# Convolution taps that read by token from SBUF, and modulation steps outside the down-products, in a two-block transformer kernel

## The chip, the cores and the metric

The kernel runs on one core of one Trainium2 chip. The metric is the device time of one execution in microseconds, as a median over runs. Before the change it is 2077.81 us (three runs, 2076.61 to 2079.95). One more execution was recorded with a profile; its own time is in the table below.

## The reference

Everything is float32, 256 tokens of width 2048. The first block is attention and a gated MLP with a causal depthwise convolution of width 3 between its two products. The second block is modulated: one vector c gives six vectors of 2048 through the matrix w_ada (2048 x 12288), and a second vector c_ctx gives the two that the context needs. Cut to what matters here:

```
def rmsnorm(x, g):                                   # rms_norm alike
    return x * rsqrt(mean(x * x, -1) + EPS) * g

def causal_dwconv(u, w, b):                          # CONV_WIDTH = 3
    up = jnp.pad(u, ((0, 0), (CONV_WIDTH - 1, 0), (0, 0)))
    y = b
    for kk in range(CONV_WIDTH):
        y = y + up[:, kk:kk + S] * w[kk]
    return y

# first block: x (1, 256, 2048), D_FF = 5632
h = rmsnorm(x, pre_mix_g); proj = h @ w_in           # sliding-window and forgetting attention on proj
x = x + rmsnorm(mix @ w_out, post_mix_g)
h = rmsnorm(x, pre_ffn_g)
u = causal_dwconv(h @ w_up, conv_w, conv_b)          # 2 x 5632 wide
gate, val = jnp.split(u, 2, axis=-1)
y = (gelu(gate, approximate=True) * val) @ w_down
x = x + rmsnorm(y, post_ffn_g)

# second block
m = silu(c) @ w_ada + b_ada                          # 6 x 2048; c_ctx alike for ctx
h  = rms_norm(x, norm_attn_w) * (1 + sc_a) + sh_a
hc = rms_norm(ctx, norm_attn_w) * (1 + csc_a) + csh_a
x = x + g_a * (concat([attention(h, hc), pool(h)]) @ w_out)
hm = rms_norm(x, norm_mlp_w) * (1 + sc_m) + sh_m
x = x + g_m * (square(relu(hm @ w_mlp_up)) @ w_mlp_down)
return rms_norm(x, final_norm_w)
```

## The kernel before, in words

**Groups.** All large products run one after the other on TensorE (PE). The program is a list of groups, each a product of the activations with one column stripe of one weight matrix: the first block's projections, wo_a and wo_b (its output product), up0 to up10 (w_up, 1024 columns each, 512 of the gate and 512 of the value), dn0, dn2, ... dn8 (w_down), then the second block: ckv and kv, q, u, wo2 and the MLP's mup and mdn. A down-product takes two halves of 1024 output columns, called dn00 and dn01 for dn0. The order is up0, up1, up2, dn0, up3, up4, dn2, up5, up6, dn4, up7, up8, dn6, up9, up10, dn8: a down-product follows two up groups, so the last of them has its convolution while the down-product runs. Within a group one unit is one block of 128 weight rows. An up group has 16 units; a half of dn0 to dn6 has 8, a half of dn8 has 12. The last block of a group is made one output bank after the other, so the weights of its last unit are wanted earlier than its place says.

**Three passes and the split.** Each product is made in three passes, high x high, high x low and low x high. The weights arrive as 1 MB transfers of two units from the queue of SP into one of four buffers `raw`; ACT writes the high part (L190, `hi`, four buffers), and VectorE (DVE) the rest (L202, `lo` = raw - hi, four buffers, 128x1024 per unit). So DVE must make one `lo` per unit, and PE waits where it is late.

**Side work.** After each unit `tick()` issues one more step of the side work of the group before (a list given to `later`), and on the ticks that the table `PACE` names one step of `ada_side()`, the modulation. Such a step is one pass of DVE over 128 rows of w_ada, multiplied with silu(c) and summed: L641 for c, L638 for c_ctx (only for the first 32 of 96 row blocks). There are 128 of them in the program. The rows come through the same SP queue into the same four `raw` buffers, 1 MB each, and the load for the next step is issued with the L641 step before. A down-product's groups had fill steps at ticks 5, 8 and 2, 5, 8 of their halves.

**The convolution.** `up(g).after` holds it. PE's products stand in four PSUM banks per group with the tokens in an order in which even and odd ones alternate (`evens` reads them back). For each of 8 blocks of 128 channels ACT multiplies by the last tap and adds the bias (L1002, PSUM to SBUF), and DVE adds the two others with L1006 on all but the first tokens that the shifted view reaches, and with L1009 on 1 or 2 columns left over: 16 of L1006 and 16 of L1009 per up group. Then gelu (L1014, ACT), the product (L1017, DVE) and the split of the result (L1023 ACT, L1024 DVE). L1036 and L1038 add the down-products to the block's sum.

**What sets the order.** Within one engine instructions run in a fixed order, and the order is made ahead of time by a list scheduler from the steps as they are issued. An instruction that waits holds all behind it on its engine. Tiles come from pools that rotate: `P4` (p4) has 10 buffers of 4096 bytes per partition. It holds the tap results, the split results and the junk output of L638.

**Warm-up.** `warm_mix` (L356 to L372) issues 60 matmuls (10 on each of six operand pairs) ahead of up0 and 30 ahead of the second block's mup0, while PE waits for a norm. Their result is not used.

## Time and profile before

| | |
|---|---|
| median of three runs | 2077.81 us (2076.61 to 2079.95) |
| profiled execution, its own time | 2074.69 us |
| its span in the trace | 2072.9 us |
| PE busy | 2030.2 us, 98% |
| DVE busy | 1594.8 us, 77% |
| ACT busy | 1078.6 us, 52% |
| POOL busy | 40.4 us, 2% |

The span runs from the first to the last instruction of the profiled execution; 1.8 us of the execution's time lie outside of it. A view of groups gives, for each kind of instruction, the sum of the busy time, the mean duration of one, and behind the second bar the idle time of the engine ahead of them with what ended it. The timeline gives an instruction's start and duration, and in brackets the idle time ahead of it. A duration is longer than the distance to the next start, since instructions of one engine overlap a little at their ends: a `lo` shows as 1.22 us and is followed after 1.14.

### The profile page before, as it was taken

Reading aid. Unit: us, or ns where it says so; the run is one execution under the profiler, and the core shown is the slowest. Engines: PE = TensorE matmul, PEld = TensorE weight load, DVE = VectorE, ACT = ScalarE, POOL = GpSimd, SP = SyncE. Lnnn points to the kernel's source line nnn. Section 1 sums busy time; section 2 is a strip of 40 time slices with the busy share of each in tenths; the row PEclk is TensorE's granted clock in tenths of the full one; section 3 lists DMA queues with packets and bytes.
Section 4 is the critical chain, followed back from the end, with each engine's and each line's share of the span. In section 5 each row is a group of like instructions: output and inputs, shape, how many; then the busy total and the mean of one; then the engine's idle time right before and its main releaser. Section 6 shows DMA issues by size and latency. Waiting matters only on the chain.

```text
span 2072.9 us, 35204 instructions
## 1 busy us (share of the span) xinstructions
PE 2030.2 (98%) x14344; PEld 1885.6 (91%) x14344; DVE 1594.8 (77%) x2271; ACT 1078.6 (52%) x1559; POOL 40.4 (2%) x58
## 2 busy tenths in 40 slices
PE   8999999999999999999999999999999999999997
PEld 7998988998998999989889978889999999999986
DVE  6787788799789788897899798876657667566577
ACT  5556575555454554545557467455544434444444
POOL 0001000000000000000000000000000000000000
PEclk9999999999999999999999999999999999999999
DMA  8753676566767779888887854765667676666673
GB/s 310 283 192 136 162 226 242 209 245 244 274 236 253 276 267 333 292 310 292 284 291 249 310 189 143 200 186 192 234 246 264 224 277 238 216 204 203 202 241 106
DMA packets 120961, 491.39 MB, mean 237 GB/s; under 512 B 8736, under 2 KB 12640, under 8 KB 107360
## 3 DMA queue, kind: packets, MB, share of 16 engines
q1 hardware_dynamic: 120800, 489.16, 68.4%
q8 instruction: 112, 1.84, 0.3%
q14 instruction: 49, 0.40, 0.1%
HBM read 484.90 MB, written 2.13 MB: 235 GB/s over the span
## 4 chain that ended last, share of the span: by engine, by line
PE 85%; DVE 8%; DMA 3%; ACT 2%; issue 2%; POOL 0%; POOLq 0%; ACTq 0%; SPq 0%; DVEq 0%
PE b_up L326 21%; PE b_mup L326 17%; PE b_mdn L326 16%; PE b_dn L326 5%; PE b_qk L326 4%; PE b_wo_a L326 4%; DVE lo L202 3%; PE b_v L326 2%; DMA raw<-in_w_ada 2%; PE b_qa L326 2%; PE b_q L326 2%; PE b_wo_p L326 2%; PE b_wo_b L326 2%; PE b_u L326 1%; DVE raw L641 1%
## 5 line engine op out<-in xcount | busy, mean ns | idle before, releaser
L190 ACT CAST hi<-raw 128x1024 fp32r<-128x1024 f32 (+2 forms) x716 | 726.9, 1027 | 724.7 <-PE b_mup L326 166.7
L202 DVE TENSOR_TENSOR lo<-raw,hi 128x1024 fp32r<-128x1024 f32 (+2 forms) x716 | 845.7, 1198 | 314.1 <-ACT hi L190 311.1
L326 PE MATMUL b_up<-a,hi 128*128 128x256 f32 x2816 | 473.7, 276 | 0.0
L326 PEld LDWEIGHTS b_up<-a,hi 128*128 128x128 f32 x2816 | 428.9, 192 | 0.2
L326 PE MATMUL b_up<-a,lo 128*128 128x256 f32 x1408 | 387.2, 275 | 0.0
L326 PE MATMUL b_mup<-a,hi 128*128 128x256 f32 x2048 | 344.4, 275 | 1.3 <-ACT a L428 1.3
L326 PEld LDWEIGHTS b_mup<-a,hi 128*128 128x128 f32 x2048 | 311.3, 192 | 2.0 <-ACT a L428 1.6
L326 PE MATMUL b_mdn<-hi,p 128*128 128x512 f32 x1024 | 304.7, 379 | 0.0
L326 PE MATMUL b_mup<-a,lo 128*128 128x256 f32 x1024 | 281.5, 275 | 0.0
L326 PEld LDWEIGHTS b_up<-a,lo 128*128 128x128 f32 x1408 | 270.5, 192 | 0.0
L641 DVE SCALAR_TENSOR_TENSOR raw<-raw,srow 128x2048 f32<-128x2048 f32 x96 | 219.5, 2286 | 58.2 <-DMA raw<-in_w_ada 58.2
L326 PEld LDWEIGHTS b_mdn<-hi,p 128*128 128x128 f32 x1024 | 193.0, 189 | 27.1
L326 PE MATMUL b_dn<-hi,p 128*128 128x512 f32 x704 | 210.9, 383 | 0.0
L326 PEld LDWEIGHTS b_mup<-a,lo 128*128 128x128 f32 x1024 | 196.6, 192 | 0.0
L326 PE MATMUL b_mdn<-lo,p 128*128 128x512 f32 x512 | 194.0, 379 | 0.0
L326 PEld LDWEIGHTS b_dn<-hi,p 128*128 128x128 f32 x704 | 133.9, 191 | 18.8
L326 PE MATMUL b_dn<-lo,p 128*128 128x512 f32 x352 | 134.9, 386 | 10.6 <-DVE lo L202 10.6
L326 PEld LDWEIGHTS b_mdn<-lo,p 128*128 128x128 f32 x512 | 96.8, 189 | 13.7
L638 DVE SCALAR_TENSOR_TENSOR p<-raw,srow 128x2048 bf16<-128x2048 f32 x32 | 73.2, 2289 | 22.0 <-DMA raw<-in_w_ada 22.0
L326 PE MATMUL b_qk<-a,hi 128*128 128x256 f32 x512 | 89.7, 280 | 0.0
L326 PEld LDWEIGHTS b_dn<-lo,p 128*128 128x128 f32 x352 | 67.1, 191 | 23.8 <-DVE lo L202 14.3
L1006 DVE SCALAR_TENSOR_TENSOR p<-b_up,vecs,p 128x254 f32<-128x254 f32 (+1 forms) x176 | 82.2, 472 | 1.0 <-ACT p L1002 0.9
(263 smaller groups left out, 2568.2 us busy)
## 6 DMA issues: line engine op xcount, KB each, us to landing
raw<-in_w_ada SPq DMA_DIRECT2D x96, 1024.0 KB, 6.6
raw<-in_w_up SPq DMA_DIRECT2D x88, 1024.0 KB, 5.0
raw<-in_w_mlp_up SPq DMA_DIRECT2D x64, 1024.0 KB, 5.0
raw<-in_w_mlp_down SPq DMA_DIRECT2D x64, 1024.0 KB, 5.5
raw<-in_w_in SPq DMA_DIRECT2D x50, 1024.0 KB, 6.0
raw<-in_w_down SPq DMA_DIRECT2D x44, 1024.0 KB, 6.6
raw<-in_w_out SPq DMA_DIRECT2D x32, 512.0 KB, 6.7
raw<-in_w_out SPq DMA_DIRECT2D x16, 1024.0 KB, 6.4
```

Source lines behind the costliest of these rows:

```text
L190: nc.scalar.copy(h, r)
L202: self.dve.tensor_tensor(out=l, in0=r, in1=h.bitcast(F32), op=ALU.subtract)
L326: self.mm = self.pe.matmul(dst, lhsT, rhs, start=first and n == 0 and m == 0, stop=last and n == len(prog) - 1 and m == 2, skip_group_chec ...
L638: self.dve.scalar_tensor_tensor(out=junk, in0=r, scalar=1.0, in1=self.srow[1], op0=ALU.mult, op1=ALU.mult, accum_out=self.adac[:, f:f + 1])
L641: self.dve.scalar_tensor_tensor(out=r, in0=r, scalar=1.0, in1=self.srow[0], op0=ALU.mult, op1=ALU.mult, accum_out=self.ada[:, f:f + 1])
L1006: self.dve.scalar_tensor_tensor(out=o, in0=evens(p)[:, :, 0:128 - n], scalar=cw(t, 2 - n), in1=o, op0=ALU.mult, op1=ALU.add)
```

## The change

Three things change together.

1. `PACE`: the down-products dn0 to dn8 have no fill ticks any more; the odd ups from up3 have seven (4, 6, ... 16) in place of three, the even ones six in place of five. The number of fill ticks between up0 and dn8 falls from 72 to 68; what is left of the modulation runs in later groups, as it did.
2. The convolution: ACT copies each up group's four banks to two SBUF tiles of 4 x 258 columns by token (`take`, four instructions per group), whose first two columns POOL has set to zero. ACT's first tap and both DVE taps read there, at whole width. The 16 instructions on 1 or 2 columns go, and the banks are free after the copies. p4 gets 12 buffers of 4128 bytes (10 x 4096 before).
3. `warm_mix`: the same number of matmuls, 60 and 30, with other stationary operands (strided by 4, 8 and 16 columns, one column broadcast, shifted slices) and one moving operand for all.

```diff
@@ -31,8 +31,8 @@
 
 
 PACE = dict(v=3, kva=3, qa=4, qk=5, wo_a=2, wo_b=3, ckv=99, kv=2, u=6, q=7, wo2_p=2, wo2_a=99, mup=99, mdn=4)
-PACE.update({f"up{i}": (6, 8, 12, 13, 16) if i < 2 else (7, 10, 15) if i % 2 else (8, 9, 11, 13, 15) for i in range(11)})
-PACE.update({f"dn{i}{half}": ((5, 8), (2, 5, 8))[half] for i in range(0, 10, 2) for half in range(2)})
+PACE.update({f"up{i}": (6, 8, 12, 13, 16) if i < 2 else (4, 6, 8, 10, 12, 14, 16) if i % 2 else (8, 9, 10, 11, 13, 15) for i in range(11)})
+PACE.update({f"dn{i}{half}": () for i in range(0, 10, 2) for half in range(2)})
 
 
 WARM = dict(up0=0, mup0=1)
@@ -114,7 +114,7 @@
         self.raw_p = P("raw", 4)
         self.w_p = P("w", 4)
         self.a8_p = P("a8", 8)
-        self.p4_p = P("p4", 10)
+        self.p4_p = P("p4", 12)
         self.row_p = P("row", 1)
         self.dram_p = P("dram", 1, space=bass.MemoryType.DRAM)
         self.p2_p = P("p2", 6)
@@ -362,10 +362,9 @@
 
         bk = self.bank("warm")
         x = x.rearrange("p k t -> p (k t)")
-        w = x[:, 1024:1152]
-        at = lambda o, d: x[:, o:o + 2 * d].rearrange("p (a b) -> p b a", a=2)[:, 0:128]
-        kinds = (((w, at(0, 128)), (w, at(0, 256)), (w, at(16, 128)), (w, at(48, 128)), (w, at(0, 512)), (x[:, 1024:1280:2], at(0, 128))),
-                 ((w, at(8, 128)), (w, at(0, 136)), (w, at(0, 192))))[kind]
+        w = ((x[:, 1024:1536:4], x[:, 1024:2048:8], x[:, 0:2048:16], x[:, 1024:1025].to_broadcast([128, 128]), x[:, 1028:1156], x[:, 1032:1160]),
+             (x[:, 1040:1168], x[:, 1056:1184], x[:, 0:1920:15]))[kind]
+        kinds = [(v, halves(x[:, 0:256])) for v in w]
         with self.tc.issue_after(after.ins):
             for lhsT, rhs in kinds:
                 for _ in range(10):
@@ -993,20 +992,25 @@
                 gs[g] = out = [None, None]
                 gv = []
 
+                ps = []
+
+                def take(i):
+
+                    if not ps:
+                        ps.extend(self.P4([128, 4, 258]) for _ in range(2))
+                        for t in ps:
+                            nc.gpsimd.memset(t[:, :, 0:2], 0.0)
+                    for t, bank in zip(ps, (banks[i // 2], banks[2 + i // 2])):
+                        ac.copy(t[:, i:i + 2, 2:258].rearrange("p j (a b) -> p j a b", a=2), evens2(bank))
+
                 def taps(s, i):
                     if not gv:
                         gv.extend(self.P4([128, 4, 256]) for _ in range(2))
                     t = 44 * s + 4 * g + i
-                    p = banks[2 * s + i // 2][:, 256 * (i % 2):256 * (i % 2) + 256]
-                    d = gv[s][:, i]
-                    ac.activation(rows2(d), evens(p), AF.Identity, scale=cw(t, 2), bias=cw(t, 3))
+                    p, d = ps[s][:, i], gv[s][:, i]
+                    ac.activation(d, p[:, 2:258], AF.Identity, scale=cw(t, 2), bias=cw(t, 3))
                     for n in (1, 2):
-
-                        o = rows2(d)[:, :, n:128]
-                        self.dve.scalar_tensor_tensor(out=o, in0=evens(p)[:, :, 0:128 - n], scalar=cw(t, 2 - n), in1=o,
-                                                      op0=ALU.mult, op1=ALU.add)
-                        o = d[:, 128:128 + n]
-                        self.dve.scalar_tensor_tensor(out=o, in0=evens(p)[:, 0, 128 - n:128], scalar=cw(t, 2 - n), in1=o,
+                        self.dve.scalar_tensor_tensor(out=d, in0=p[:, 2 - n:258 - n], scalar=cw(t, 2 - n), in1=d,
                                                       op0=ALU.mult, op1=ALU.add)
 
                 def act(i):
@@ -1023,7 +1027,8 @@
                     ac.copy(hi, val)
                     self.dve.tensor_tensor(out=lo, in0=val, in1=hi.bitcast(F32), op=ALU.subtract)
 
-                self.later(*[lambda i=i: (taps(0, i), taps(1, i)) for i in range(4)],
+                take(0)
+                self.later(*[lambda i=i: (i or take(2), taps(0, i), taps(1, i)) for i in range(4)],
                            *[lambda f=f, i=i: f(i) for i in (0, 2) for f in (act, split)])
             return Group(f"up{g}", 16, 1024, self.loader(a["w_up"], 0, 1024 * g, 1024), a_banks(8), lambda k: ht["xs"](k),
                          before=up_before if g == 0 else None, prep=(lambda b: ht["need"](b + 3)) if g == 0 else None,
```

In the changed kernel the lines move a little: `lo` stays L202, the modulation steps are L637 and L640, the taps L1011 (ACT) and L1013 (DVE).

**DVE where dn0 begins, before.** `lo_5481` is the first `lo` of dn0, `lo_5512` the second; `adac` and `ada` mark modulation steps, `b_up` taps of up2:

```order
L638 SCALAR_TENSOR_TENSOR p_763_5449,adac<-raw_5389,srow_353 128x2048
L202 TENSOR_TENSOR lo_5481<-raw_5332,hi_5455 128x1024
L641 SCALAR_TENSOR_TENSOR raw_5389,ada<-raw_5389,srow_385 128x2048
L202 TENSOR_TENSOR lo_5512<-raw_5332,hi_5483 128x1024
L1006 SCALAR_TENSOR_TENSOR p_784_5582<-b_up_5011,vecs,p_784_5582 128x2x127
L1009 SCALAR_TENSOR_TENSOR p_784_5582<-b_up_5011,vecs,p_784_5582 128x1
L1006 SCALAR_TENSOR_TENSOR p_784_5582<-b_up_5011,vecs,p_784_5582 128x2x126
L1009 SCALAR_TENSOR_TENSOR p_784_5582<-b_up_5011,vecs,p_784_5582 128x2
L1006 SCALAR_TENSOR_TENSOR p_784_5582<-b_up_5012,vecs,p_784_5582 128x2x127
L1009 SCALAR_TENSOR_TENSOR p_784_5582<-b_up_5012,vecs,p_784_5582 128x1
```

The same place after the change (`lo_5468` and `lo_5498` are the first two of dn0):

```order
L637 SCALAR_TENSOR_TENSOR p_762_5375,adac<-raw_5345,srow_353 128x2048
L202 TENSOR_TENSOR lo_5468<-raw_5316,hi_5442 128x1024
L640 SCALAR_TENSOR_TENSOR raw_5345,ada<-raw_5345,srow_385 128x2048
L637 SCALAR_TENSOR_TENSOR p_774_5496,adac<-raw_5436,srow_353 128x2048
L202 TENSOR_TENSOR lo_5498<-raw_5316,hi_5470 128x1024
L1013 SCALAR_TENSOR_TENSOR p_791_5576<-p_776_5524,vecs,p_791_5576 128x256 x4
L202 TENSOR_TENSOR lo_5554<-raw_5379,hi_5532 128x1024
L202 TENSOR_TENSOR lo_5556<-raw_5379,hi_5534 128x1024
L1013 SCALAR_TENSOR_TENSOR p_792_5577<-p_777_5525,vecs,p_792_5577 128x256
```

Two modulation steps of dn0 now stand ahead of the second `lo`; before, one stood there and another behind the seventh. The taps are one instruction each, and `lo` stand between them.

**SP around the change from up9 to up10, before.** A row is a 1 MB transfer, `in_w_ada` one of the modulation, `in_w_up` one of two units of weights:

```order
L628 DMA raw_10199<-in_w_ada 128x2048
L390 DMA raw_10203<-in_w_up 128x2x1024
L390 DMA raw_10261<-in_w_up 128x2x1024
L628 DMA raw_10290<-in_w_ada 128x2048
L390 DMA raw_10322<-in_w_up 128x2x1024
L390 DMA raw_10380<-in_w_up 128x2x1024
L628 DMA raw_10437<-in_w_ada 128x2048
L390 DMA raw_10465<-in_w_up 128x2x1024
L390 DMA raw_10503<-in_w_up 128x2x1024
L390 DMA raw_10583<-in_w_up 128x2x1024
```

After the change:

```order
L389 DMA raw_10183<-in_w_up 128x2x1024
L627 DMA raw_10212<-in_w_ada 128x2048
L389 DMA raw_10244<-in_w_up 128x2x1024
L627 DMA raw_10273<-in_w_ada 128x2048
L389 DMA raw_10305<-in_w_up 128x2x1024
L627 DMA raw_10334<-in_w_ada 128x2048
L627 DMA raw_10391<-in_w_ada 128x2048
L389 DMA raw_10399<-in_w_up 128x2x1024
L389 DMA raw_10437<-in_w_up 128x2x1024
L389 DMA raw_10511<-in_w_up 128x2x1024
```

Among ten transfers four are now the modulation's, one to one with the weights' and the last two next to each other; before there were three, with two of the weights between them.

**DVE where dn6 begins, before.** `lo_9576` and `lo_9607` are its first two, `lo_9655` and `lo_9657` the next:

```order
L641 SCALAR_TENSOR_TENSOR raw_9482,ada<-raw_9482,srow_385 128x2048
L202 TENSOR_TENSOR lo_9576<-raw_9425,hi_9550 128x1024
L647 TENSOR_TENSOR ada<-ada,vecs 128x16
L202 TENSOR_TENSOR lo_9607<-raw_9425,hi_9578 128x1024
L1006 SCALAR_TENSOR_TENSOR p_1255_9675<-b_up_9103,vecs,p_1255_9675 128x2x127
L1009 SCALAR_TENSOR_TENSOR p_1255_9675<-b_up_9103,vecs,p_1255_9675 128x1
L641 SCALAR_TENSOR_TENSOR raw_9544,ada<-raw_9544,srow_385 128x2048
L1006 SCALAR_TENSOR_TENSOR p_1255_9675<-b_up_9103,vecs,p_1255_9675 128x2x126
L1009 SCALAR_TENSOR_TENSOR p_1255_9675<-b_up_9103,vecs,p_1255_9675 128x2
L1006 SCALAR_TENSOR_TENSOR p_1256_9676<-b_up_9105,vecs,p_1256_9676 128x2x127
L1009 SCALAR_TENSOR_TENSOR p_1256_9676<-b_up_9105,vecs,p_1256_9676 128x1
L202 TENSOR_TENSOR lo_9655<-raw_9486,hi_9635 128x1024
```

After the change (`lo_9515`, `lo_9546`, `lo_9600`, `lo_9602` are the first four):

```order
L202 TENSOR_TENSOR lo_9515<-raw_9361,hi_9489 128x1024
L640 SCALAR_TENSOR_TENSOR raw_9390,ada<-raw_9390,srow_385 128x2048
L640 SCALAR_TENSOR_TENSOR raw_9422,ada<-raw_9422,srow_385 128x2048
L646 TENSOR_TENSOR ada<-ada,vecs 128x16
L202 TENSOR_TENSOR lo_9546<-raw_9361,hi_9517 128x1024
L1013 SCALAR_TENSOR_TENSOR p_1274_9622<-p_1261_9572,vecs,p_1274_9622 128x256 x4
L202 TENSOR_TENSOR lo_9600<-raw_9426,hi_9580 128x1024
L202 TENSOR_TENSOR lo_9602<-raw_9426,hi_9582 128x1024
L640 SCALAR_TENSOR_TENSOR raw_9483,ada<-raw_9483,srow_385 128x2048
L1013 SCALAR_TENSOR_TENSOR p_1275_9623<-p_1262_9573,vecs,p_1275_9623 128x256 x3
L202 TENSOR_TENSOR lo_9630<-raw_9487,hi_9606 128x1024
```

Three modulation steps now stand ahead of the fifth `lo`, where one stood behind the second and another further down, behind the seventh.

## Rows read from the trace of the kernel before

**Rows 1.** The page: engines, and the chain that ended last.

```profile
PE 2030.2 (98%) x14344; PEld 1885.6 (91%) x14344; DVE 1594.8 (77%) x2271; ACT 1078.6 (52%) x1559; POOL 40.4 (2%) x58
PE 85%; DVE 8%; DMA 3%; ACT 2%; issue 2%; POOL 0%; POOLq 0%; ACTq 0%; SPq 0%; DVEq 0%
```

**Rows 2.** Windows (us; busy PE, PEld, DVE, ACT, POOL; PEclk, DMA): dn0–dn8, mdn.

```profile
496.15:542.32 46.17, 43.67 (x195) 37.33 (x193) 43.22 (x66) 25.25 (x33) 0.00 (x0) 0.96 0.73 260
628.08:671.02 42.94, 41.71 (x195) 36.21 (x193) 42.80 (x68) 22.06 (x27) 0.00 (x0) 1.00 0.72 247
756.78:800.16 43.38, 41.70 (x194) 36.21 (x193) 41.38 (x64) 21.21 (x26) 0.00 (x0) 1.00 0.82 299
885.92:928.31 42.39, 41.71 (x194) 36.22 (x193) 41.15 (x66) 21.48 (x26) 0.00 (x0) 1.00 0.82 301
1014.07:1087.48 73.41, 68.47 (x323) 58.37 (x322) 67.11 (x105) 43.88 (x71) 3.31 (x2) 0.98 0.83 281
1556.96:1598.40 41.44, 41.44 (x195) 36.29 (x193) 31.29 (x31) 19.70 (x21) 0.00 (x0) 1.00 0.73 264
```

**Rows 3.** The same view of up4 and up7.

```profile
585.20:628.08 42.88, 42.88 (x387) 42.88 (x386) 37.15 (x53) 21.29 (x26) 0.00 (x0) 1.00 0.64 233
800.16:843.04 42.88, 42.88 (x385) 42.87 (x384) 33.25 (x39) 18.69 (x21) 0.00 (x0) 1.00 0.87 315
```

**Rows 4.** Timeline of PE where dn0, dn4, dn8 and ckv wait.

```profile
515.71 0.48 PE L326 MATMUL b_dn<-lo,p 128*128 128x512 f32 x1 [1.89 <-DVE lo L202]
517.83 1.06 PE L326 MATMUL b_dn<-hi,p 128*128 128x512 f32 x2
775.46 0.48 PE L326 MATMUL b_dn<-lo,p 128*128 128x512 f32 x1 [1.68 <-DVE lo L202]
1035.93 0.79 PE L326 MATMUL b_dn<-lo,p 128*128 128x512 f32 x1 [3.13 <-DVE lo L202]
1089.90 0.38 PE L326 MATMUL b_ckv<-a,lo 128*128 128x256 f32 x1 [2.04 <-DVE lo L202]
```

**Rows 5.** Timeline of DVE in dn4 ahead of its eighth lo.

```profile
771.46 0.47 DVE L1006 SCALAR_TENSOR_TENSOR p<-b_up,vecs,p 128x252 f32<-128x252 f32 x1
771.85 0.21 DVE L1009 SCALAR_TENSOR_TENSOR p<-b_up,vecs,p 128x2 f32<-128x2 f32 x1
771.98 2.28 DVE L641 SCALAR_TENSOR_TENSOR raw<-raw,srow 128x2048 f32<-128x2048 f32 x1
774.18 1.22 DVE L202 TENSOR_TENSOR lo<-raw,hi 128x1024 fp32r<-128x1024 f32 x1
```

**Rows 6.** Groups of instructions by line and shape.

```profile
L202 DVE TENSOR_TENSOR lo<-raw,hi 128x1024 fp32r<-128x1024 f32 x668 | 805.8, 1221 | 298.7 <-ACT hi L190 295.7
L641 DVE SCALAR_TENSOR_TENSOR raw<-raw,srow 128x2048 f32<-128x2048 f32 x96 | 219.5, 2286 | 58.2 <-DMA raw<-in_w_ada 58.2
L1006 DVE SCALAR_TENSOR_TENSOR p<-b_up,vecs,p 128x254 f32<-128x254 f32 x88 | 41.4, 473 | 1.0 <-ACT p L1002 0.9
L1038 DVE TENSOR_TENSOR a<-b_dn,a 128x512 f32<-128x512 f32 x32 | 21.0, 680 | 0.0
L946 DVE TENSOR_TENSOR a<-a,p 128x512 f32<-128x512 f32 x16 | 10.8, 685 | 0.9 <-ACT p L474 0.6
L1002 ACT ACTIVATE p<-b_up,vecs 128x256 f32<-128x256 f32 x88 | 48.5, 563 | 54.0 <-DVE p L1009 37.6 <-PE b_up L326 16.2
L1256 ACT COPY p<-b_aux 128x512 f32<-128x512 f32 x32 | 18.7, 584 | 9.3 <-PE b_aux L1254 8.9
L372 PE MATMUL b_warm<-a 128*128 128x256 f32 x90 | 10.4, 276 | 0.0
```

**Rows 7.** A window inside dn8, columns as in Rows 2.

```profile
1070.00:1087.00 17.00, 17.00 (x80) 14.69 (x79) 13.71 (x18) 6.52 (x9) 0.85 (x1) 1.00 0.96 348
```

**Rows 8.** DMA rate in 40 equal slices of 585 to 630 us (up4).

```profile
GB/s 426 84 0 69 288 426 149 0 200 404 324 15 58 251 404 222 0 0 124 364 426 433 408 390 397 248 22 0 117 335 324 302 320 379 320 419 255 40 0 73
```

**Rows 9.** DMA issues of w_up: count, size, median us from issue to landing.

```profile
raw<-in_w_up SPq DMA_DIRECT2D x88, 1024.0 KB, 5.0
```

## Prediction

> **What bounds the kernel now.** I read the page's busy times and its chain first: PE is busy 98% of the span and 85% of the chain is PE's; DVE holds 8%, DMA 3% [rows 1]. So only stretches in which PE waits can give time back. The windows by group come next. An mdn, the second block's down-product with the same 192 matmuls, takes 41.44 us, all of it PE. dn0, dn2, dn4 and dn6 take 46.17, 42.94, 43.38 and 42.39: 4.73, 1.50, 1.94 and 0.95 too much, 9.12 us in all. dn8 has 288 matmuls, 41.44 x 1.5 = 62.16, and takes 73.41: 11.25 more, of which 4.94 is idle PE (73.41 - 68.47) and the rest transposes and slower matmuls. In these windows DVE is busy 41.15 to 43.22 us out of 42 to 46, in the mdn 31.29 [rows 2]. The up groups lose nothing: each of up3 to up10 takes 42.88 with PE busy throughout, and DVE has 5.7 (up4) to 15 us left [rows 3]. The timeline of PE names who is late: every wait shown ends with `lo` [rows 4]. What stood ahead of that `lo` is in DVE's timeline: a run of taps, then a modulation step of 2.20 us, then `lo` [rows 5]. So the down-products are short of DVE time ahead of the last `lo` of their first half, and the ups have it to spare.
>
> **Part 1: the taps.** From start to start a tap takes 0.39 us and the small one behind it 0.13 [rows 5]. Sixteen small ones go per up group: 16 x 0.13 = 2.1 us of DVE in each stretch behind an up, 11 x 2.1 = 23 us in all. The large tap grows from 254 to 256 columns and reads SBUF where it read PSUM. For that the trace has a pair: adding 512 columns took 680 ns with a PSUM operand and 685 ns from SBUF [rows 6]. So I take 0.39 us, between 0 and +0.08 for a second tap that follows its first at once (the overlap of 0.473 to 0.39 lost): 8 x 0.08 = 0.6 us per group at most.
>
> [...]
>
> ACT gets four copies of 512 columns per group at 584 ns, 2.3 us, and its taps read SBUF at about the old 563 ns [rows 6]. ACT is busy 21 to 25 us of 42 to 46 [rows 2], so the copies hide. They are quick to free the bank, and the 37.6 us in which ACT's taps waited for the small DVE taps [rows 6] go; ACT was not late for PE. The two small memsets per group fall to POOL, busy 2% [rows 1]; at its mean, 40.4 / 58 = 0.7 us, they are done long before the copies.
>
> **Part 2: the modulation leaves the down-products.** A step is 2.20 us of DVE and a 1 MB transfer. What counts is how many stand ahead of a half's last `lo`. By DVE's order before and after, in the first halves: dn0 two and two (its third comes behind), dn2 two and one, dn4 two and two, dn6 two and three, dn8 two and three ahead of the eighth `lo`. The fill ticks are gone, but steps issued at an up's last ticks slide in behind the first `lo` of the down-product, as the order of dn0 and dn6 shows above. In the second halves: 3, 3, 2, 2, 3 before, 0, 1, 0, 1, 0 after. Term by term, in us:
> - dn0: 2.1 us less tap work ahead of a `lo` that was 1.89 late [rows 4]. The stall goes, and with it the stretch behind it where matmul pairs took 1.06 us and the window's clock fell to 0.96 [rows 2, 4]. That is nearly the whole 4.73; I take -3.5 (0 to -4.7), since two steps now come at once near its start.
> - dn2: 2.1 + 2.2 less ahead of a lateness of 1.50: -1.5 (0 to -1.5).
> - dn4: 2.1 less against 1.68 [rows 4], but its two steps now stand side by side and the second can wait for its transfer: -1.2 (0 to -1.9).
> - dn6: 2.2 more and 2.1 less: 0 (-0.9 to +2).
> - dn8: in the first half the same balance, so the 3.13 [rows 4] stays; in the second three steps go, 6.6 us: -1.5 (-4.9, all of its idle time, to +1).
> - ckv: its 2.04 wait for `lo` [rows 4] follows a crowded DVE; no step stands there any more: -0.9 (0 to -2.0).
>
> **Part 3: what the ups and later groups get.** The even ups' DVE work grows most. up4 had four steps and gets seven, 6.6 us, less 2.1 for taps that run beside it: 37.15 + 6.6 - 2.1 = 41.7 of 42.88 [rows 3]. This is full, but fits. up6, up8 and up10 get five or six. Price in waits: 0 to +6 (a wait of 1.5 in each of four); I take +0.8. Outside, the steps left over go to the second block's output product, three into a half that had none: stalls that steps made before were 1.7 to 3.1 [rows 4], and I take +0.5 (0 to +2).
>
> **Part 4: the warm-up.** Numbers of matmuls are unchanged. All 90 took 276 ns on average [rows 6], ten of them with a stride of 2 on the stationary side. Strides of 4 to 16 and the broadcast are not in the trace. Fifty of the 90 have one now. In an up group 384 matmuls of this shape take 42.88 us, 0.112 each [rows 3]; if those fifty took twice as long, 50 x 0.112 = 5.6 us, of which the wait for the norm hides a part: +4 at most. I take 0, the nearest row. It could be a gain too, up to -1, if PE came out of it at a higher clock than before.
>
> **Sum.** -3.5 - 1.5 - 1.2 + 0 - 1.5 - 0.9 + 0.8 + 0.5 = -7.3 us. Against the profiled execution's own 2074.69 us this is 2067.4. The median of the runs shown is 2077.81, 3.1 above that execution, and the changed kernel will be timed as a median too: 2070.5 us.
>
> **Rivals.**
>
> *A, the stalls only move (2076 us).* Steps that slide in at the start of dn4, dn6 and dn8 come in pairs behind the first `lo`, so `lo` four is late where `lo` eight was. Only dn0 and dn2 gain, dn0 half of it: -1.8 - 1.5, with +0.8 and +0.5 as above: -2.0, thus 2075.8. For it: the DVE work ahead of the last `lo` of dn6 and dn8 doesn't shrink. Against it: four `lo` buffers let DVE run ahead, and the second halves lose eleven steps, 24 us.
>
> *B, slower: the transfers in the ups (2085 us).* In the ups weights and modulation now alternate, 2.1 MB per two units of 2.68 us: 391 GB/s. The window inside dn8 moved 348 with the engines at 0.96 [rows 7]. At 348 a pair takes 6.03 us against 5.36, and seven of them put an odd up 4.7 us behind. In the even ups four ticks in a row ask for 4 + 2 MB in 10.7 us; at 348 these take 18.1, 7.4 us behind. The lead is four buffers of 2.68 us less 5.0 for landing [rows 9] and 2.2 for the split, about 3.5 us. Then each of the four even ups waits 3.9, and the 0.8 of my sum goes: 15.6 - 0.8 = +14.8, thus 2085.3 (with 1.2 in each odd up as well, 2090). It is slower than before by more than 4.2 us once the even ups wait 3.1 each, a lag of 6.6: 6.3 MB in 17.3 us, so from 363 GB/s down. Against it: slices of 1.1 us inside up4 reach 408 to 433 GB/s [rows 8]. At 427 a pair takes 4.9 us, and the four ticks in a row 14.7, 4.0 behind: a wait of 0.5.
>
> [...]
>
> *C, all stalls go (2062 us).* dn0 to dn6 come to 41.44 (-9.1), dn8 loses its idle 4.9 and ckv 2.0, with nothing lost in the ups: -16, 2074.69 - 16 + 3.1 = 2062. For it: DVE is relieved of 23 us of taps. Against: three steps ahead of dn6's and dn8's `lo`.
>
> *D, the warm-up costs.* +4 on the sum, 2074.5: the change would be hardly seen.
>
> **How the numbers follow.** My forecast 0.50, A 0.17, B 0.13, C 0.12, D 0.08. The forecast's own range is 2066 to 2074. The range for 8 in 10 reaches to 2062 (half of C left out) and 2081 (A and D inside, most of B out). Under 0.2%, 4.2 us, this measurement can't tell a change from none; so faster means below 2073.7, slower above 2082.0. Faster: C, most of the forecast and a little of D, 0.58. Same: A, the rest of those and a part of B, 0.30. Slower: 0.12.
>
> **What would show it.** Right: windows of dn0 and dn2 at 41.5 to 42.7, dn4 below 43, ups still 42.88; DVE busy in dn0 about 43.2 - 2 x 2.2 - 2.1 = 36.7; the new taps at a mean near 473 ns; no PE wait at ckv. Wrong: PE waits inside up8 or up10 ended by `lo` with DVE waiting for `in_w_ada` ahead of it (B), waits moved to the fourth or fifth unit of dn6 and dn8 (A), more than 3.5 us for 30 warm-up matmuls (D). If the taps from SBUF run well above 0.39 us apart, part 1's gain is not there, and dn0 and dn4 keep their stalls.

## The result and the profile after

The changed kernel takes 2091.5 us (median of four runs, 2086.86 to 2093.27) against 2077.99 for the kernel before (four runs): a ratio of 1.0063, 95% interval 1.0048 to 1.0078. It is slower by 13.5 us where 7.3 less were forecast, and lies outside the range. The profiled execution took 2092.33 us, with a span of 2090.5, 17.6 more than before; the account by place goes by these two spans.

The page answers to [rows 1]. PE's number of matmuls is unchanged, but it is busy 10 us longer: the warm-up takes 4.7 us more, and matmuls behind some of the waits are slower (the granted clock was 0.50 for 3.4 us in dn4 and for 6.8 us in wo2_a). In the chain PE has lost 7 points, and DMA has gained 5:

```profile
PE 2040.3 (98%) x14344; PEld 1889.7 (90%) x14344; DVE 1574.6 (75%) x2095; ACT 1098.2 (53%) x1603; POOL 42.1 (2%) x80
PE 78%; DVE 8%; DMA 8%; issue 4%; ACT 3%; POOL 0%; SPq 0%; POOLq 0%; ACTq 0%; DVEq 0%
```

The windows by group come next, in the columns of [rows 2]: dn0, dn2, dn4, dn6 and dn8 (an mdn takes 41.45 us here).

```profile
495.08:537.10 42.02, 41.88 (x195) 35.99 (x193) 32.84 (x41) 25.21 (x34) 0.21 (x2) 1.00 0.80 262
622.86:665.92 43.06, 42.22 (x194) 36.07 (x193) 37.97 (x50) 21.36 (x27) 0.21 (x2) 1.00 0.76 259
751.68:798.69 47.01, 43.39 (x194) 37.42 (x193) 38.94 (x50) 21.67 (x26) 0.21 (x2) 0.96 0.82 279
886.89:933.27 46.38, 42.82 (x194) 35.84 (x193) 40.05 (x53) 23.05 (x29) 0.21 (x2) 1.00 0.86 302
1021.92:1096.49 74.57, 67.56 (x322) 57.13 (x321) 62.47 (x90) 46.64 (x77) 2.37 (x2) 1.00 0.78 266
```

dn0 went from 46.17 to 42.02 us, as forecast. dn4 and dn6 went the other way, to 47.01 and 46.38. In both, DVE is *less* busy than before (38.94 and 40.05 us against 41.38 and 41.15). In dn4 3.62 us of the 47.01 are idle PE; the rest of its excess is mostly slower matmuls behind the wait, for from 762.18 to 765.60 the granted clock was 0.50 of full speed, where it was 1.00 from 757.45 to 762.18 and again from 765.60 to 768.00. The next rows are the pairs up7 with up8 and up9 with up10 (85.76 when PE never waits), and wo2_a, the last 1024 of 2048 weight rows of the second block's output product (41.44 before):

```profile
798.69:886.89 88.20, 87.08 (x769) 86.12 (x768) 67.60 (x71) 42.54 (x53) 0.21 (x2) 1.00 0.78 282
933.27:1021.92 88.65, 86.80 (x770) 86.06 (x769) 67.43 (x71) 42.69 (x53) 0.00 (x0) 1.00 0.78 282
1341.45:1390.33 48.88, 44.94 (x193) 37.70 (x192) 32.82 (x37) 16.61 (x24) 0.00 (x0) 0.93 0.93 251
```

The account, after less before, in us by PE's starts of groups, with the forecast in brackets: dn0 -4.1 (-3.5), dn2 +0.1 (-1.5), dn4 +3.6 (-1.2), dn6 +4.0 (0), dn8 +1.2 (-1.5), ckv -2.7 and kv -0.9 (-0.9 together), the two late pairs of ups +5.3 (+0.8), wo2_a +7.4 and the stretch from its end through mup0 +4.8 (+0.5 together), wo_b with the first warm-up -0.7, the rest -0.5. But for rounding that is +17.6.

PE's timeline names what it waited for, in dn4, wo2_a and ahead of mup0; the last two rows are the second warm-up and mup0's first product. In the late ups it waits for `lo` too, up to 1.26 us at a time, and the wait at ckv has shrunk to 0.69:

```profile
761.07 0.48 PE L326 MATMUL b_dn<-lo,p 128*128 128x512 f32 x1 [3.62 <-DVE lo L202]
1360.65 1.22 PE L326 MATMUL b_wo_a<-hi,a 128*128 128x512 f32 x2 [3.49 <-ACT hi L190]
1390.33 4.69 PE L371 MATMUL b_warm<-a 128*128 128x256 f32 x30
1400.82 1.22 PE L326 MATMUL b_mup<-a,hi 128*128 128x256 f32 x4 [1.16 <-ACT a L427]
```

dn4's wait comes in the group's third unit, where the kernel before waited in the eighth: near rival A's place. Ahead of it stands this in DVE's timeline, in one run but for the short rows that read a step's sum; the first two `lo` are of dn4's first transfer of weights, the `lo` of 759.80 are of its second:

```profile
747.68 2.29 DVE L640 SCALAR_TENSOR_TENSOR raw<-raw,srow 128x2048 f32<-128x2048 f32 x1 [2.00 <-DMA raw<-in_w_ada]
749.90 1.22 DVE L202 TENSOR_TENSOR lo<-raw,hi 128x1024 fp32r<-128x1024 f32 x1
751.04 2.29 DVE L640 SCALAR_TENSOR_TENSOR raw<-raw,srow 128x2048 f32<-128x2048 f32 x1
753.25 1.22 DVE L202 TENSOR_TENSOR lo<-raw,hi 128x1024 fp32r<-128x1024 f32 x1
754.39 2.85 DVE L1013 SCALAR_TENSOR_TENSOR p<-p,vecs,p 128x256 f32<-128x256 f32 x7
757.58 2.29 DVE L640 SCALAR_TENSOR_TENSOR raw<-raw,srow 128x2048 f32<-128x2048 f32 x1 [0.34 <-DMA raw<-in_w_ada]
759.80 2.35 DVE L202 TENSOR_TENSOR lo<-raw,hi 128x1024 fp32r<-128x1024 f32 x2
```

From 745.68, where the `lo` before it ends, to 761.02 are 15.3 us, and DVE finished three `lo` in them. Three modulation steps took 6.7 of these, their waits for their rows 2.3 (2.00 and 0.34), seven taps 2.9 and the three `lo` 3.4. The first of the three had its high part at 746.23 and began at 749.90, held behind the step that waited for its row. See also SP's queue in the same microseconds (start, length, transfer), and then ACT:

```profile
753.36 0.38 SPq L389 DMA_DIRECT2D raw<-in_w_down  x1
759.91 2.65 SPq L389 DMA_DIRECT2D raw<-in_w_down  x2
```

```profile
752.99 1.99 ACT L190 CAST hi<-raw 128x1024 fp32r<-128x1024 f32 x2 [1.36 <-DMA raw<-in_w_down]
760.68 1.04 ACT L190 CAST hi<-raw 128x1024 fp32r<-128x1024 f32 x1 [3.73 <-DMA raw<-in_w_down]
```

The `lo` that PE waited for had its weights in time: ACT made the high parts of both its units from 752.99 to 754.98, and only DVE's taps and step kept it back. The wait in dn4 is one of DVE's order.

The buffers act beside this. The step of 751.04 ends at 753.33, and at 753.36 SP issues a transfer of w_down, into the buffer that the step has just freed. ACT can begin to split it at 760.68, after 3.73 us with nothing to split. The step of 757.58 ends at 759.87, and SP's next transfer goes out at 759.91. A step's own row waits alike: that of 757.58 was issued at 750.01, as the step of 747.68 ended. So loads of weights and of rows are issued as DVE's steps and `lo` end, since all share four `raw` buffers in rotation. In dn4 PE did not have to wait for the late weights as well; elsewhere it did for a little (0.56 us in dn6's fifth unit, 0.67 and 0.56 in dn8's). Over the span these waits of ACT were 22.6 us for w_down and 11.2 for w_up in the kernel before; now:

```profile
ACT hi L190 <- DMA raw<-in_w_down: 37.7, 12, 7.0
ACT hi L190 <- DMA raw<-in_w_out: 15.6, 3, 11.5
ACT hi L190 <- DMA raw<-in_w_up: 12.9, 3, 6.0
```

Last the instructions of the change, answering to [rows 6]:

```profile
L1013 DVE SCALAR_TENSOR_TENSOR p<-p,vecs,p 128x256 f32<-128x256 f32 x176 | 74.0, 476 | 0.0
L1011 ACT ACTIVATE p<-p,vecs 128x256 f32<-128x256 f32 x88 | 47.8, 597 | 0.8
L1004 ACT COPY p<-b_up 128x512 f32<-128x512 f32 x44 | 25.1, 576 | 3.3 <-PE b_up L326 3.2
```

The taps from SBUF take 476 ns and the copies 576, close to what was taken from [rows 6] (473 and 584); ACT's taps take 597, 34 more than taken. For DVE's taps part 1 of the prediction was right: 473 ns from PSUM with 254 columns, 476 from SBUF with 256.

### The profile page after: what moved, and what is told of

It is laid out like the page before. It is cut to its first block, busy times and chain, and to the rows that moved or that the text cites. A ratio compares the mean times of both kernels' runs of the same rounds, so it can differ in the third digit from the quotient of the medians.

```text
span 2090.5 us, 35098 instructions
## 1 busy us (share of the span) xinstructions
PE 2040.3 (98%) x14344; PEld 1889.7 (90%) x14344; DVE 1574.6 (75%) x2095; ACT 1098.2 (53%) x1603; POOL 42.1 (2%) x80
## 4 chain that ended last, share of the span: by engine, by line
PE 78%; DVE 8%; DMA 8%; issue 4%; ACT 3%; POOL 0%; SPq 0%; POOLq 0%; ACTq 0%; DVEq 0%
PE b_mup L326 16%; PE b_mdn L326 16%; PE b_up L326 14%; PE b_dn L326 8%; DMA raw<-in_w_ada 5%; PE b_qk L326 4%; DVE lo L202 3%; PE b_v L326 2%; PE b_qa L326 2%; PE b_q L326 2%; PE b_wo_a L326 2%; PE b_wo_p L326 2%; PE b_u L326 1%; DMA raw<-in_w_down 1%; ACT hi L190 1%
## 5 line engine op out<-in xcount | busy, mean ns | idle before, releaser
L202 DVE TENSOR_TENSOR lo<-raw,hi 128x1024 fp32r<-128x1024 f32 (+2 forms) x716 | 844.3, 1198 | 332.0 <-ACT hi L190 330.0
L640 DVE SCALAR_TENSOR_TENSOR raw<-raw,srow 128x2048 f32<-128x2048 f32 x96 | 219.7, 2288 | 63.8 <-DMA raw<-in_w_ada 63.3
L637 DVE SCALAR_TENSOR_TENSOR p<-raw,srow 128x2048 bf16<-128x2048 f32 x32 | 73.3, 2289 | 27.8 <-DMA raw<-in_w_ada 27.8
L326 PE MATMUL b_wo_a<-hi,a 128*128 128x512 f32 x256 | 78.4, 393 | 3.9 <-ACT hi L190 3.9
```

Of the source, the lines that this page charges most:

```text
L202: self.dve.tensor_tensor(out=l, in0=r, in1=h.bitcast(F32), op=ALU.subtract)
L326: self.mm = self.pe.matmul(dst, lhsT, rhs, start=first and n == 0 and m == 0, stop=last and n == len(prog) - 1 and m == 2, skip_group_chec ...
L637: self.dve.scalar_tensor_tensor(out=junk, in0=r, scalar=1.0, in1=self.srow[1], op0=ALU.mult, op1=ALU.mult, accum_out=self.adac[:, f:f + 1])
L640: self.dve.scalar_tensor_tensor(out=r, in0=r, scalar=1.0, in1=self.srow[0], op0=ALU.mult, op1=ALU.mult, accum_out=self.ada[:, f:f + 1])
```

## The experiments

Theory 1: the new table costs, since it crowds the modulation's transfers and steps into places without room. Rival 2: the taps and copies cost. Rival 3: the warm-up's strided operands cost. Within theory 1, later kernels vary bytes, DVE's time and buffers. Each kernel gets a new order from the scheduler, and the place of the steps changes with it; where that matters it is said. Each ratio is to the kernel before on the same chip, with its 95% interval.

**Taps and warm-up, old table.**

```diff
-PACE.update(... (4, 6, 8, 10, 12, 14, 16) if i % 2 else (8, 9, 10, 11, 13, 15) ...)
-PACE.update({f"dn{i}{half}": () for i in range(0, 10, 2) for half in range(2)})
+PACE.update(... (7, 10, 15) if i % 2 else (8, 9, 11, 13, 15) ...)
+PACE.update({f"dn{i}{half}": ((5, 8), (2, 5, 8))[half] for i in range(0, 10, 2) for half in range(2)})
```

> The changed kernel with the kernel before's table of fill ticks; the taps, the copies, p4 and the warm-up are the changed ones. Theory 1 (the new table is what costs: it puts the modulation's transfers one to one between the weights', and its four fewer ticks force steps into wo2_a): faster than before, 2066 to 2072 us; dn0, dn2 and dn4 near 41.5 to 42.5, all up groups 42.88, wo2_a 41.44. Rival 2 (the taps cost: copies and taps from SBUF make ACT and DVE late): slower than before, 2085 or more, with waits left in dn4 and dn6. Rival 3 (the warm-up costs): 3 us above what the taps alone take.

2069.3 us, 0.9968 (0.9957 to 0.9980): faster than before by 0.3%, as theory 1 said. Windows of dn2, dn4, and up7 with up8:

```profile
624.24:669.56 45.32, 42.51 (x194) 35.97 (x193) 43.72 (x56) 21.36 (x27) 0.21 (x2) 1.00 0.73 243
755.32:796.76 41.44, 41.44 (x194) 36.29 (x193) 39.52 (x51) 21.45 (x26) 0.21 (x2) 1.00 0.90 330
796.76:882.52 85.76, 85.76 (x770) 85.76 (x768) 65.84 (x72) 44.28 (x56) 0.21 (x2) 1.00 0.83 290
```

dn4 has no wait left, and up7 with up8 and wo2_a (41.44) are whole. Not as expected are dn2 (45.32, four waits for `lo` of 0.25 to 1.48 us in the new order), dn0 (43.23), up3 with up4 (86.10) and up9 with up10 (86.89). The taps and copies are not what costs.

**Taps alone**, with the old `warm_mix` as well.

> Taps, copies and p4 of the change alone; the table of fill ticks and the warm-up are those of before. Theory 1: faster than before, 2066 to 2072. Rival 2: as slow as the changed kernel, 2085 or more. Rival 3 (the strided warm-up costs about 3 us ahead of mup0): about 3 us faster than the kernel with taps and new warm-up; if its longer run at up0 gives back what it costs at mup0, the two are equal within 1 us.

2071.55 us, 0.9976 (0.9961 to 0.9991). The interval overlaps the one above, and the kernel with the strided warm-up is if anything the faster one, so rival 3 falls.

**The table alone**, in the kernel before.

> The new table of fill ticks alone; taps and warm-up are those of before. Theory 1: slower than before by at least as much as the changed kernel, 2090 to 2105, with waits inside up8 and up10, dn4 and dn6 at 46 us or more, and wo2_a at 48 or 49. Rival 2: no slower than before, 2070 to 2080. Rival 3: as rival 2.

2087.25 us, 1.0052 (1.0034 to 1.0069): slower, if less than the 2090 expected. dn4, up7 with up8, and wo2_a (dn6 took 45.50):

```profile
754.34:800.40 46.06, 43.01 (x194) 35.81 (x193) 41.78 (x68) 21.65 (x26) 0.00 (x0) 1.00 0.85 304
800.40:886.76 86.36, 86.16 (x769) 85.90 (x768) 70.17 (x89) 40.40 (x47) 0.00 (x0) 1.00 0.81 292
1338.11:1385.76 47.65, 43.81 (x193) 36.75 (x192) 32.82 (x37) 16.47 (x24) 0.00 (x0) 0.96 0.95 259
```

The two down-products and wo2_a are late as in the changed kernel, without its taps and with the old warm-up. The pairs of ups are nearly whole here (86.36, and 85.76 for the other), and this expectation missed.

**More fill ticks in q.** One number: `q=7` becomes `q=3`.

> The changed kernel with a fill tick in q every third unit in place of every seventh, so that no modulation step is left for wo2_a. Theory 1, its second half (the steps forced into wo2_a hold its raw buffers, and the product's banks end together so that the norm ahead of mup0 comes late): wo2_a back at 41.44, mup0's first product about 7 us after wo2_a's end in place of 10.5; in all -8 to -11, 2080 to 2083. If wo2_a was late for another reason: no change, 2089 to 2093. If only the strided warm-up delays mup0: wo2_a at 41.44 but 10 us to mup0, 2083 to 2085.

2091.57 us, 1.0075 (1.0060 to 1.0090): no gain. But wo2_a is back at 41.44 and mup0's first product comes 8.6 us behind it in place of 10.5. What was gained there was lost in u, 104.20 us after 93.15: its attention chain runs through DVE, and five steps begin in it, two in the changed kernel. The longest of PE's waits in u is 2.17 us, for DVE's L1243.

So the steps left over do cost about what the account says (wo2_a and mup0 together 10.8 us less), and q's and u's side of the program is no place for them.

**One tick in each second half**, `((), (5,))[half]` for the down-products.

> The changed kernel with one fill tick in the second half of each of the five down-products, so that nothing is left for wo2_a, q and u keep their ticks. If the steps left over are what costs 10 us at wo2_a and mup0 and a second half has room: wo2_a 41.44, mup0's first product 7 to 8 us behind it, u 93.3, ups and first halves as in the changed kernel; 2079 to 2083. If any place for four more steps costs as much as wo2_a did: 2088 to 2092.

2082.6 us, 1.0027 (1.0015 to 1.0039), inside the first case: wo2_a 41.45, mup0 after 7.3 us, u 93.5. dn4 and dn6 stay at 47.80 and 46.52, the late pairs at 88.67 and 88.80. By the two ratios 7.5 of the 13.5 us, give or take 4, go with the steps that were left over; by the traces wo2_a and mup0 gave 12 back, and other groups took a part of it.

**Small transfers, full steps.** The load is cut, and the step multiplies the same columns again.

```diff
-                self.nc.sync.dma_start(out=t[:, :D], in_=self.a["w_ada"][128 * f:128 * f + 128])
+                self.nc.sync.dma_start(out=t[:, 2048:2080], in_=self.a["w_ada"][128 * f:128 * f + 128, 0:32])
...
-            self.dve.scalar_tensor_tensor(out=r, in0=r, scalar=1.0, in1=self.srow[0],
+            self.dve.scalar_tensor_tensor(out=r, in0=q, scalar=1.0, in1=w[0],
```

> The changed kernel whose modulation loads 32 of 2048 columns of each 128 rows (16 KB in place of 1 MB) and multiplies these again and again, so that DVE's steps keep their 2.2 us and nearly all bytes of the modulation are gone; the modulation vectors are therefore others. Theory 1, transfers (the modulation's 1 MB between the weights' make DVE and the weights wait): dn4 and dn6 fall from 47.0 and 46.4 to 43 or less, up7 with up8 and up9 with up10 from 88.2 and 88.7 to 85.8, wo2_a from 48.9 to 41.4; in all 2060 to 2070 us. Theory 1, DVE time (the steps themselves are too many ahead of the low parts): dn4, dn6 and the ups stay within 1 us, only wo2_a falls; 2080 or more.

2076.12 us, 0.9987 (0.9972 to 1.0002), between the two. dn4, and up7 with up8:

```profile
757.57:799.01 41.44, 41.44 (x195) 36.29 (x193) 32.68 (x42) 21.10 (x26) 0.21 (x2) 1.00 0.72 240
799.01:890.01 91.00, 87.92 (x770) 87.53 (x768) 75.17 (x83) 45.19 (x56) 0.21 (x2) 0.98 0.52 171
```

dn4 and dn6 (41.44 both) and wo2_a (41.65) are whole or nearly so, and dn8 falls to 67.50, as the transfers' side said. But the new order also took steps out of the down-products. What DVE spent on L640's steps (L643 here) in dn4, in the changed kernel, in this one, and in the one with five buffers further down:

```profile
751.68:798.69 47.01, 6.24 (x6) 0.96 0.82 279
757.57:799.01 41.44, 2.04 (x2) 1.00 0.72 240
751.02:793.45 42.43, 3.05 (x4) 1.00 0.81 275
```

So dn4's cure is no proof that bytes did the harm there. The ups get worse, 91.00 for the pair, as neither side said: over a third of the bytes are gone (171 GB/s after 282), DVE's steps are not, and more of them stand there (27.6 us in the pair after 22.4). So lateness in the ups is no matter of bytes per second. And DVE still waited 75 us for the modulation's rows in all, 91 with 1 MB, so its bytes are not the greater part of that waiting.

**Short steps, full transfers.** `[:, 0:256]` on operands and result of both steps.

> The changed kernel whose modulation still loads all of its 1 MB per step, but multiplies only 256 of 2048 columns, 0.35 us of DVE in place of 2.2; the modulation vectors are therefore others. Transfers: dn4, dn6 and the ups lose less than half of their excess, wo2_a stays at 47 to 49; 2076 us or more. DVE time: dn0 to dn6 at 41.5 to 42, ups 85.76 a pair, wo2_a as late as before or not, 2058 to 2068.

2052.81 us, 0.9885 (0.9863 to 0.9908), by two runs; a step took 0.42 us. dn4, up7 with up8, and wo2_a:

```profile
745.13:786.58 41.45, 41.45 (x195) 36.30 (x194) 31.56 (x44) 21.32 (x26) 0.21 (x2) 1.00 0.86 293
786.58:872.33 85.75, 85.75 (x769) 85.75 (x768) 54.83 (x82) 44.41 (x56) 0.22 (x2) 1.00 0.86 315
1306.01:1349.94 43.93, 41.97 (x193) 36.03 (x192) 27.22 (x35) 16.69 (x24) 0.00 (x0) 1.00 0.92 265
```

Every down-product to dn6 is at 41.45, dn8 at 66.06, each pair of ups at 85.75, with all transfers in place and the new table of ticks. Only wo2_a (43.93) and mup0's start behind it (10.5 us) are still late. Two steps begin in dn4 and eleven in up7 with up8, as many as in the changed kernel or one more, so here the cure is not that they went elsewhere. DVE's 2.2 us per step are behind nearly all of the lateness in ups and down-products, the old one too; the bytes alone stop nothing outside wo2_a.

**Five raw buffers** in the changed kernel: `P("raw", 5)`, and `P("p4", 10)` for the room.

> The changed kernel with five raw buffers in place of four (p4 has 10 buffers in place of 12 to make room). If the four buffers are the limit (a step's transfer goes out only when VectorE has freed a buffer, and VectorE reaches the step before it has landed): VectorE's waits for in_w_ada fall from 91 us to under 50, dn4 and dn6 to 43 or less, the pairs of ups to 86.5 or less, and the time to 2076 to 2082, wo2_a still late. If VectorE's 2.2 us a step are the limit by themselves: the waits for in_w_ada fall, but lows are as late as now, 2088 to 2092. If p4 with 10 makes new waits: 2092 or more.

2073.15 us, 0.9988 (0.9977 to 0.9999): by the medians 18 us faster than the changed kernel, more than expected. dn4, up9 with up10, and wo2_a:

```profile
751.02:793.45 42.43, 41.96 (x195) 36.14 (x193) 35.75 (x48) 21.32 (x26) 0.21 (x2) 1.00 0.81 275
924.48:1015.00 90.52, 87.81 (x769) 87.53 (x768) 73.04 (x76) 45.09 (x56) 0.21 (x2) 0.98 0.82 297
1326.49:1368.34 41.85, 41.71 (x193) 36.21 (x192) 31.01 (x36) 16.49 (x24) 0.00 (x0) 1.00 0.97 279
```

dn4 is at 42.43, dn8 at 66.50, and wo2_a at 41.85. In the view of waits ACT's waits for w_down and w_up are gone, and those for w_out are 3.6 us. DVE's waits for the modulation's rows, though, fell only from 91 to 79 us (expected: under 50). It looks as if the cure came through the weights; but here too the order took steps out of dn4 (3.05 us after 6.24), out of dn8 and one out of wo2_a, and put them into the ups, where what is left is: twelve begin in up9 with up10 (90.52), ten in the changed kernel. What the buffer did and what the order did is not told apart by this run.

**The old table with five**, and its control with four raw and ten p4 buffers.

> Taps and warm-up of the change, the old table of fill ticks, five raw buffers and 10 of p4. If the buffers limit: dn2 from 45.3 to 43 or less and the other stalls of the first halves shrink, 2062 to 2066. If VectorE's time limits: as with four, 2067 to 2072.

> Taps and warm-up of the change, the old table, four raw buffers, 10 buffers of p4 in place of 12. If the two more buffers of p4 are needed: slower than with 12 by 2 us or more, 2072 or above. If not: 2067 to 2072, and the difference of the two kernels with five raw buffers is theirs alone.

2071.9 us, 0.9985 (0.9974 to 0.9996), and 2067.65 us, 0.9960 (0.9947 to 0.9974). With the old table p4 needs no 12 buffers. Five raw buffers gave nothing here, they cost 4 us by the medians: the scheduler's order changed with them, dn2 fell to 42.26, but dn4 went to 46.92 with DVE busy for 43.28 of it, and dn8 to 77.12.

**A table between the two**, with four and with five raw buffers: odd ups `(5, 8, 11, 15)`, first halves `(8,)`, second halves `(2, 5, 8)`, dn81 `(2, 5, 8, 11)`.

> Taps and warm-up of the change with a table between the two: one fill tick in each first half of a down-product (before two), three in the second halves (four in dn8's), four in the odd ups from up3 (before three, changed seven), five in the even ones. If only bursts of one transfer to one cost and DVE time in the first halves still matters: a little faster than with the old table, 2064 to 2068. If the old table's stalls were left only by chance: the same, 2068 to 2071. If any step moved into an up costs there what it gives back: 2071 to 2078.

> Taps and warm-up of the change, five raw buffers, 10 of p4, and the table between the two (one fill tick in each first half, three in the second halves, four in odd ups, five in even ones). In VectorE's order one modulation step stands ahead of the eighth low part in the first halves of dn0, dn4, dn6 and dn8 and none in dn2, and none is left for wo2_a. If both VectorE's time in the first halves and the buffers decide: every down-product to dn6 at 42.5 or less, dn8 at 70 or less, pairs of ups at 86.5 or less, wo2_a 41.44; 2058 to 2066 us. If a better place in one group is always paid in the next: 2067 to 2073, as the others.

2070.16 us, 0.9968 (0.9955 to 0.9982), and 2076.78, 0.9998 (0.9985 to 1.0011). The first does no better than the old table. The second missed its range by 10 us: DVE waited 128 us for the modulation's rows (79 in the changed kernel with five), dn4 and dn6 took 45 us and dn8 76.56. So of three tables the fifth buffer helped with one, the changed one, and cost 4 to 7 us with the other two.

## Why the prediction was wrong

**The reading of the bound was right.** In the up and down groups PE still waits for `lo`, as in [rows 4].

What it drew from this, that the ups have DVE time to spare, held for up3 to up6 and not for up7 to up10.

**Part 1, the taps, was right.** DVE's busy time fell by 20 us where 23 were counted. The taps alone gain 0.24% and with the warm-up 0.32%. That this is near the forecast for the whole change (2069.3 and 2070.5) is chance, since the forecast was added up from other places.

**Part 4, the warm-up, was right for the time.** It took 0, and the medians show nothing, though 40 of the 90 matmuls took twice as long, 4.7 us in all; its estimate, should fifty do so, was 5.6.

**Part 2 failed at dn4, dn6 and dn8.** It counted DVE's microseconds ahead of the *last* `lo` of a half, "two and two", "two and three" steps at 2.2 us, as if the groups' `lo` before it had time to spare. The short steps show that DVE's time is behind the lateness. But the changed order puts the steps in a run around the head of the group, and the rows of dn4 above show the price: 15.3 us for three `lo`, of which PE needs one per 2.59. The waits for the steps' rows, which the sum had named for dn4 only ("the second can wait for its transfer"), were 2.3 of this. The sum took -1.2 for dn4, 0 for dn6 and -1.5 for dn8; they measured +3.6, +4.0 and +1.2, 11.5 off together. That a step holds a buffer from the issue of its load to its end (from 740.64 to 749.98 for the step of 747.68) and so sets when other loads go out is in the rows too; how much of the stalls comes by this way stays open, since both kernels that vary it, small transfers and five buffers, moved the steps as well.

**Part 3 failed most, at wo2_a.** "+0.5 (0 to +2)" measured +7.4, and +4.8 behind it. Of the 7.4, 3.9 are idle PE and 3.5 slower matmuls: the granted clock was 0.50 from 1359.52 to 1366.34, where it had stood at 1.00 from 1341.45 to 1357.16, until the long wait. The bound came from stalls that steps had made in other groups, [rows 4]. (The late ups, +0.8 in the sum, measured +5.3, inside their own 0 to +6.) The bound did not ask what the transfers of wo2_a have to spare. In the kernel before they already ran without a pause; first a window of it in that stretch, then one of the changed kernel (columns as in [rows 2], the last two the share of the 16 DMA engines and GB/s):

```profile
1325.00:1336.00 11.00, 11.00 (x52) 9.64 (x51) 7.43 (x9) 3.78 (x4) 0.00 (x0) 1.00 1.03 221
```

```profile
1352.00:1360.00 8.00, 5.16 (x24) 4.17 (x23) 2.92 (x5) 0.45 (x1) 0.00 (x0) 0.97 1.03 217
```

The rate is 217 to 221 GB/s with the engines' share at 1.03, while wo2_a's 1024 x 2048 weights are 8.4 MB in 41.44 us, 202. Into this run of weights four more transfers of 1 MB went, at 1327.95, 1333.41 and the two of the first row here; w_out was not issued again before 1348.00:

```profile
1338.59 6.87 SPq L627 DMA_DIRECT2D raw<-in_w_ada  x2
1348.00 16.26 SPq L901 DMA_DIRECT2D raw<-in_w_out  x10
```

That could not be made up for: PE waited for a high part at 1360.65, and ACT had waited 11.5 us for the weights. This place is the transfers': with short steps wo2_a stayed late (43.93), with small transfers it did not (41.65). With five buffers three such transfers went, the last 3.2 us ahead of the group and not 3.7 us into it, and it took 41.85. Then mup0 came late for another reason: not the strided operands (the old warm-up with the new table took 9.9 us from wo2_a's end to mup0, the new one with the old table 7.2), but the order. In the new order wo2_a's four banks end close together. First and last product with the gate, before and after:

```profile
1371.84 0.69 DVE L1346 TENSOR_TENSOR p<-b_wo_a,a 128x512 f32<-128x512 f32 x1 [2.39 <-PE b_wo_a L326]
1377.67 0.69 DVE L1346 TENSOR_TENSOR p<-b_wo_a,a 128x512 f32<-128x512 f32 x1 [1.11 <-PE b_wo_a L326]
```

```profile
1387.94 0.69 DVE L1351 TENSOR_TENSOR p<-b_wo_a,a 128x512 f32<-128x512 f32 x1 [5.68 <-PE b_wo_a L326]
1392.21 0.68 DVE L1351 TENSOR_TENSOR p<-b_wo_a,a 128x512 f32<-128x512 f32 x1
```

Before, the first bank was read 5.6 us ahead of PE's end (1377.47), and the last 0.2 behind it; after, 2.4 ahead of it (1390.33) and 1.9 behind it, and the norm that follows ends later by this and by a longer wait for ACT (2.22 us after 1.02). That makes 3.5 of the 4.8 us; the other 1.4 are mup0 itself, at a granted clock of 0.97 from 1400.82 to 1445.42 (0.50 in its first 2.4 us) after 1.00. In the kernel with five buffers wo2_a was in time and mup0 still came 10.5 us after it.

**The rivals.** B, the slower one, had the right place (the ups) and near the right price (2085), but not the cause: it decided from a rate below 363 GB/s, while with 16 KB in place of 1 MB the ups were later still. Nor did the transfers stop at such a rate: the changed kernel moved 378 GB/s from 738 to 754 us, and a slice of 0.75 us there reaches 448. A named the move of the stalls to the heads of dn4 and dn6, and gave them too little. C did not come, and D was not seen in the time.

**What stays open.** Taps and table together cost more than their parts: 0.9968 x 1.0052 = 1.0020 against 1.0063 (1.0048 to 1.0078). By the traces 7.7 us are more than the parts: 3.6 of them in the late pairs of ups, 2.9 in dn4; what in the new order makes them was not separated. No run changes buffers, bytes or ticks with the order held, so what a buffer alone is worth is not shown. The changed kernel with 10 buffers of p4 and four of `raw` was not run.

## What to carry to other kernels

A group's busy time hides a run. Where side work stands in an engine's fixed order, write down the order around the head of each group and add up what stands between two pieces of the main stream; fewer microseconds in the group can still be more of them in a row. Where side work shares a rotating pool with the main stream, look also at which load waits for the buffer that it holds. Before work is put into a group, ask of that group's own rows what it has to spare, DMA too: wo2_a's weights ran one behind the other with a DMA share of 1.03, so nothing was left. And count what is taken out of a table: work that has to be done by a date is done at that date, at its price there.

## What the runs showed of the hardware

Stationary operands with a column stride of 4, 8 or 16 cost PE about twice as long per matmul of 256 columns. The first 30 matmuls of the warm-up ahead of up0, ten with each of these strides, took 6.85 us, 0.23 each; the other 30, with the broadcast and the shifted slices, 3.35 us, 0.11 (the counts take in one matmul at the edge):

```profile
351.56:358.41 6.85, 6.85 (x31) 6.85 (x31) 5.84 (x13) 6.38 (x17) 1.47 (x2) 1.00 0.01 2
358.41:361.76 3.35, 3.35 (x31) 3.35 (x31) 1.75 (x6) 3.25 (x8) 0.67 (x4) 1.00 0.00 0
364.00:370.00 6.00, 6.00 (x56) 6.00 (x55) 5.68 (x9) 5.93 (x9) 0.00 (x0) 1.00 0.41 132
```

The last row is the start of up0. In the kernel before, PE idled 2.8 us ahead of it (2.83, up to 362.64); the longer warm-up fills that time. From 364 to 370 us the granted clock was 1.00 here and 0.78 before. This gain and the longer warm-up at mup0 (4.69 us after 3.51) are too small to be seen in the medians.

The output product's weights, each transfer 512 KB to 64 partitions, move at 217 to 222 GB/s with the DMA engines' share at 1.03, in both kernels; 1 MB transfers to 128 partitions reach slices above 420 (426 and 433 in [rows 8], slices of 1.1 us). That the 64 partitions are the cause was not separated.
